# A hybrid decoder layer on one Trainium2 core: the last contraction block of the MLP's second matmul goes from plain products to seven products, and row ends move into the last product

## The chip, the cores and the metric

The kernel runs on one core of one Trainium2 chip. A core has TensorE (PE in the profile; its weight loads are PEld), VectorE (DVE), ScalarE (ACT), GpSimd (POOL) and SyncE (SP), which issues all DMAs here. PE writes its results to PSUM, of which the kernel uses eight banks of 128 partitions x 512 float32. The metric is device time in microseconds (us): the median of several executions. A profile is one more execution, taken by the hardware profiler; its span runs from the first to the last instruction.

## What is computed

One decoder layer for 1024 tokens of width 1024, all in float32. The first half (attention heads beside a gated recurrence, an output projection, a residual) is not touched by the change. The second half is the MLP:

```python
h = rmsnorm(x, mlp_pre_norm)
ff = square(relu(h @ w_ff1)) @ w_ff2        # (1024 x 1024) @ (1024 x 4096), then (1024 x 4096) @ (4096 x 1024)
x = x + rmsnorm(ff, mlp_post_norm)          # rmsnorm: y = v * rsqrt(mean(v*v) + 1e-6) * gain, row by row
```

## The kernel before

**Float32 by three passes.** Every float32 operand is split into two numbers that PE can multiply at full rate: `hi` is a copy by ACT (L83), `lo = src - hi` a subtraction by DVE (L84). A product is then three matmuls, hi x hi, hi x lo and lo x hi (`three_pass`, L86 to L89), each 128 x 128 weights against up to 512 columns.

**Seven products.** Both MLP matmuls use the Strassen-Winograd scheme: a 2 x 2 block product costs 7 block products and some block sums, not 8. The 4096 rows of `w_ff2` are eight "pairs" of 512 rows, numbered 0 to 7. For pairs 1 to 7 the first layer leaves seven left operands (blocks of the activation and their sums, made by POOL in `act_sums`) in DRAM, `act_dram[u]`, at the places `APLACE`. For pair 0 it leaves only the plain blocks (`act_plain` writes them to `act_raw`).

**Units.** A unit is one product `p` (1 to 7) of one pair: 4 row blocks x 2 contraction blocks x 3 passes = 24 matmuls (`mm2`). `GROUPS` lists the pairs that add up in the same PSUM banks: pair 1 alone, then 2, 3, 4, then 5, 6, 7. For each group the products run in the order `ORDER` (`LAST` for the last group), and for each product the pairs of the group one after the other. Four banks hold the four row blocks of a product; after its last unit `collect` takes them out: in group 0 ACT copies them to SBUF (`acc[p]`, L1640), in the others DVE adds them to `acc[p]` (L1644, L1642).

**What a unit needs.** `a_load` brings the left operand from DRAM (tile `ar`, 512 KB), `prep` splits it (`ah`, `al`) and the right one (`bh`, `bl`); `prep_sum` forms the right operand of products 5, 6, 4 and 7, one DVE operation each (L1582, L1588), from raw blocks of `w_ff2` (tile `br`, 1 MB each, two per pair; `b_load`, started by `b_pump` as buffers come free). In iteration `n` the code issues the load for unit n+3, the splits of n+2, the sum of n+4, then the matmuls of n, then a `collect` if the product ends. Each engine works strictly in this order. All second-layer tiles come from two arenas: `small` (30 slots of 128 x 1024 float32) and `large` (slots of 128 x 2048); a slot is handed out in the order in which slots were given back, and the user waits for the last reader of the old tile.

**Folding.** The seven collected sums must be combined into the four blocks of the result: C11 in `acc[2]`, C12 in `acc[3]`, C21 in `acc[4]`, C22 in `acc[7]`. These are the `fold_in` calls (L1649) in the table `at_last`, which hangs further work on the units of the last group.

**The end.** Pair 0 is multiplied plainly after the last unit: for each of the 8 row tiles and each half of the columns, 4 contraction blocks x 3 passes into a fresh bank (tile `fe`), 192 matmuls in all; its operands are loaded and split in `at_last` (`plain_load`, `plain_split`). Behind each row tile comes the row end: DVE adds the bank to `acc` (L1786), ACT squares and sums it (L1787), POOL makes the mean and the power -0.5 (L1791, L1799, L1800), DVE multiplies by the gain (L1761), and one tile later multiplies by the row's scale and adds the residual `x2r` (L1756); SP stores the row. The last tile does its second half in two quarters (L1777 to L1783).

**The first layer around it.** `ff1(q)` runs pair q = 0 to 15 of `w_ff1` by seven products; `act_store(q)` sends pair q's results to `act_dram`, two stores on SP that wait for POOL. `start2` prepares the first units during the last pair; `b_pump(-1)` and two `a_load` stand before it.

Of the kernel before, what the change touches and what calls it, by code (L numbers as in the profile page):

```python
# [35 lines left out]
def hymba_layer(ctx, tc, x, w_in, w_out, w_ff1, w_ff2, g_pre, lb_logits, g_mix, g_post,  # L36
# [1120 lines left out]
    act_raw = dp.tile([P, 2, 2, 2, 512], F32, name="actr")  # L1157
    act_dram = {u: dp.tile([P, 7, 2, 512], F32, name=f"actd{u}") for u in range(1, NPAIR // 2)}
# [145 lines left out]
    def act_plain(q):  # L1304

        l = lay.pop(q)
        nc.sync.dma_start(out=act_raw[:, q, 0, 0], in_=l["E1"][:, 0])
        nc.sync.dma_start(out=act_raw[:, q, 0, 1], in_=l["X"][:, 0])
        nc.sync.dma_start(out=act_raw[:, q, 1], in_=l["E1"][:, 1:3])
        drop(l["E1"], l["X"])  # L1310

# [180 lines left out]
    def ff1(q, between=None):  # L1492
# [9 lines left out]
        for p in EARLY if q in EARLY_PAIRS else STEADY if nq else FINAL:  # L1502
# [40 lines left out]
    GROUPS = ((1,), (2, 3, 4), (5, 6, 7))  # L1543
    NG = len(GROUPS)
    APLACE = {1: 0, 2: 1, 4: 2, 5: 3, 6: 4, 7: 5, 3: 6}
# [5 lines left out]
    acc = {}  # L1551

    def a_load(n):
        if n < n_units:
# [9 lines left out]

    b_queue = [(g, h, m) for g in range(NG) for m in range(2) for h in range(len(GROUPS[g]))]

    def b_pump(g):

        spare = sum((g, h) not in tt for h in range((len(GROUPS[g]) + 1) // 2)) if g >= 0 else 0
        while b_queue and b_queue[0][0] <= g + 1 and len(large.free) > spare:  # L1570
            b_load(*b_queue.pop(0))

# [3 lines left out]
    def b_source(g, p, h):  # L1576
# [7 lines left out]
        if p == 5 and h % 2 == 0:  # L1584
            tt[g, h // 2] = large.get(f"tt{g}{h}")
        t = tt[g, h // 2][:, 2 * (h % 2):2 * (h % 2) + 2]
        in0, in1 = {5: (b12, b11), 6: (b22, t), 4: (t, b21)}[p]
# [5 lines left out]
    def prep_sum(n):  # L1593
        if n < n_units:
            g, p, h = units[n]
            bsrc[n] = b_source(g, p, h)
            if g == NG - 1 and p == 4:
                drop(braw.pop((g, h, 1)))

    def prep(n):  # L1600
        if n >= n_units:
            return
# [20 lines left out]
    cur = []  # L1623

    def mm2(n, i, first, last):
        (ah, al), (bh, bl) = aop[n], bop[n]
        c = slice(i * P, (i + 1) * P)
        for j in range(2):
            three_pass(cur[i], (ah[:, j, c], al[:, j, c]), (bh[:, j], bl[:, j]), first and j == 0, last and j == 1)
# [4 lines left out]
    def collect(g, p, i):  # L1634

        pm = cur[i]
# [4 lines left out]
        elif g == NG - 1 and p == 4:  # L1641
            V.tensor_tensor(out=acc_at(p, i), in0=acc_at(p, i), in1=pm, op=ALU.subtract)  # L1642
# [4 lines left out]
    def fold_in(p, o, j, op=ALU.add):  # L1647

        V.tensor_tensor(out=acc[p][j], in0=acc[o][j], in1=acc[p][j], op=op)  # L1649
# [26 lines left out]
    b_pump(-1)  # L1676
# [7 lines left out]
    x2r, plain, praw = {}, {}, {}  # L1684

    def load_x2(t):
        if t < NT:
            x2r[t] = small.get(f"x2r{t}")
            nc.sync.dma_start(out=flat(x2r[t]), in_=x2_dram[t])

    def plain_load(kind, q):
        t = praw[kind, q] = large.get(f"{kind}p{q}")
        if kind == "w":
            src = w_ff2[2 * q * P:(2 * q + 2) * P].rearrange("(j p) c -> p j c", j=2)
        else:
            src = act_raw[:, q].rearrange("p j a c -> p j (a c)")
        nc.sync.dma_start(out=t.rearrange("p (j a) c -> p j (a c)", j=2), in_=src)

    def plain_split(kind, q, j):
        if j == 0:  # L1700
            plain[kind, q] = [large.get(f"{kind}p{x}{q}", F32R) for x in "hl"]
        hi, lo = (x[:, 2 * j:2 * j + 2] for x in plain[kind, q])
        split_into(hi, lo, praw[kind, q][:, 2 * j:2 * j + 2])
        if j == 1:
            drop(praw.pop((kind, q)))

    def plain_op(kind, q, j, c0, n):
        return tuple(x.rearrange("p (j a) c -> p j (a c)", j=2)[:, j, c0:c0 + n] for x in plain[kind, q])
# [3 lines left out]
        0: lambda: plain_load("w", 0),  # L1712
        1: lambda: plain_load("w", 1),
        3: lambda: fold_in(6, 1, 0),
        4: lambda: fold_in(6, 1, 1),
        5: lambda: plain_split("w", 0, 0),
        6: lambda: [fold_in(2, 1, 0), plain_split("w", 0, 1)],
        7: lambda: [fold_in(2, 1, 1), drop(*acc.pop(1))],
        8: lambda: plain_split("w", 1, 0),
        10: lambda: plain_split("w", 1, 1),  # L1720
        11: lambda: plain_load("a", 0),
        12: lambda: [fold_in(7, 6, 0), fold_in(6, 5, 0)],
        13: lambda: [fold_in(7, 6, 1), fold_in(6, 5, 1)],
        15: lambda: [fold_in(3, 6, 0), plain_split("a", 0, 0)],
        16: lambda: [fold_in(3, 6, 1), drop(*acc.pop(6)), plain_split("a", 0, 1), plain_load("a", 1)],
        18: lambda: [fold_in(4, 7, 0, ALU.subtract), plain_split("a", 1, 0), load_x2(0)],
        19: lambda: [fold_in(4, 7, 1, ALU.subtract), plain_split("a", 1, 1), load_x2(1)],
        20: lambda: [load_x2(2), load_x2(3)],
    }
    for n, (g, p, h) in enumerate(units):  # L1730
        final, nh = g == NG - 1, len(GROUPS[g])
        a_load(n + 3) if n else None
        prep(n + 2) if n else None
        prep_sum(n + 4)
        if h == 0:
            cur = [banks.get(f"f2{g}{p}{i}") for i in range(4)]
        b_pump(g)
        if final:
            at_last.get(n - n_last, lambda: None)()
        for i in range(4):  # L1740
            mm2(n, i, h == 0, h == nh - 1)
# [5 lines left out]
        if h == nh - 1:  # L1747
            for i in range(4):
                collect(g, p, i)


    def end_out(t, pieces, rf):

        xr = x2r.pop(t)
        for j, c in enumerate(pieces):
            V.scalar_tensor_tensor(c, c, rf, xr[:, j], op0=ALU.mult, op1=ALU.add)  # L1756
            nc.sync.dma_start(out=out[t * P:(t + 1) * P, j * 512:(j + 1) * 512], in_=c)
        drop(xr)

    def norm_gain(pieces, j):  # L1760
        V.tensor_tensor(out=pieces[j], in0=pieces[j], in1=gend[:, j], op=ALU.mult)  # L1761

    late = None
    for t in range(NT):
        pieces = [acc_at(p, t % 4) for p in ((2, 3) if t < 4 else (4, 7))]
        ss, rf = [col(f"fss{j}") for j in range(2)], col("frf")
        last = t == NT - 1
        for j, c in enumerate(pieces):
            pm = banks.get(f"fe{t}{j}")
            for i in range(4):  # L1770
                three_pass(pm, plain_op("a", i // 2, i % 2, t * P, P), plain_op("w", i // 2, i % 2, j * 512, 512),
                           i == 0, i == 3)
            fd = half(f"fd{t}{j}")
            if last and j:
                norm_gain(pieces, 0)
# [97 lines left out]
```

## Time and profile before

| | us |
|---|---|
| three runs | 1264.53, 1264.64, 1265.26 |
| median | 1264.64 |
| the profiled execution | 1262.62 |
| its span | 1260.6 |
| second layer, first to last matmul, of it | 943.8 to 1253.0 |

The profile groups instructions by line, engine and shape: `xN` is their number, then the busy time, the mean duration of one in ns, and the idle time of the engine before them with what ended it. The durations of matmuls overlap, so what one costs is the distance between starts. Rows of the timeline give start, duration, engine, line, operation, output and inputs. Rows of windows give for each stretch the busy time and number of instructions of PE, PEld, DVE, ACT and POOL, PE's granted clock, the mean busy share of the DMA engines and GB/s. "A <- B" among the waits is A waiting for B: us in total, times, longest.

### The profile page before, as it was taken

Reading aid. Unit: us, or ns where it says so; the run is one execution under the profiler, and the core shown is the slowest. Engines: PE = TensorE matmul, PEld = TensorE weight load, DVE = VectorE, ACT = ScalarE, POOL = GpSimd, SP = SyncE. Lnnn points to the kernel's source line nnn. Section 1 sums busy time; section 2 is a strip of 40 time slices with the busy share of each in tenths; the row PEclk is TensorE's granted clock in tenths of the full one; section 3 lists DMA queues with packets and bytes.
Section 4 is the critical chain, followed back from the end, with each engine's and each line's share of the span. In section 5 each row is a group of like instructions: output and inputs, shape, how many; then the busy total and the mean of one; then the engine's idle time right before and its main releaser. Section 6 shows DMA issues by size and latency. Waiting matters only on the chain. (4 is left out here: it accounts for less than half of the span.)

```text
span 1260.6 us, 17260 instructions
## 1 busy us (share of the span) xinstructions
PE 1235.9 (98%) x6512; PEld 1055.5 (84%) x6512; DVE 886.4 (70%) x1535; ACT 531.8 (42%) x970; POOL 300.9 (24%) x303
## 2 busy tenths in 40 slices
PE   9999999999999998999999999999999999999997
PEld 8898989888888887878878788888878888888886
DVE  5686868575666667668769756666675777698966
ACT  7623232222555556665565322222236444344412
POOL 0000000012222224046250487656621000000012
PEclk9999999999999999999999999999999999999999
DMA  5201111122322223235242545435368454424423
GB/s 210 68 18 51 34 51 34 35 84 64 88 70 82 69 83 109 103 134 183 96 155 77 207 167 184 148 133 180 142 253 324 164 201 134 160 92 133 163 88 117
DMA packets 58578, 153.98 MB, mean 122 GB/s; under 512 B 4992, under 2 KB 12928, under 8 KB 58240
## 3 DMA queue, kind: packets, MB, share of 16 engines
q1 hardware_dynamic: 58496, 152.89, 35.3%
q8 instruction: 51, 0.84, 0.3%
q14 instruction: 31, 0.25, 0.1%
HBM read 106.73 MB, written 39.85 MB: 116 GB/s over the span
## 5 line engine op out<-in xcount | busy, mean ns | idle before, releaser
L89 PE MATMUL f<-bh,al 128*128 128x512 f32 x392 | 152.6, 389 | 0.0
L88 PE MATMUL f<-bl,ah 128*128 128x512 f32 x392 | 152.6, 389 | 0.0
L87 PE MATMUL f<-bh,ah 128*128 128x512 f32 x392 | 152.6, 389 | 0.0
L84 DVE TENSOR_TENSOR al<-ar,ah 128x1024 fp32r<-128x1024 f32 x49 | 60.6, 1237 | 47.9 <-ACT ah L83 17.5
L89 PEld LDWEIGHTS f<-bh,al 128*128 128x128 f32 x392 | 73.6, 188 | 15.4
L88 PEld LDWEIGHTS f<-bl,ah 128*128 128x128 f32 x392 | 73.6, 188 | 15.3
L87 PEld LDWEIGHTS f<-bh,ah 128*128 128x128 f32 x392 | 73.6, 188 | 15.1
L83 ACT ACTIVATE ah<-ar 128x1024 fp32r<-128x1024 f32 x49 | 52.1, 1064 | 49.1 <-PE f L89 17.6
L1791 POOL TENSOR_SCALAR fp<-fss 128x1 f32<-128x1 f32 x8 | 3.7, 461 | 269.4 <-ACT fd L1787 269.4
L719 DVE TENSOR_TENSOR ptl<-pt,pth 128x512 fp32r<-128x512 f32 (+2 forms) x96 | 50.4, 552 | 23.0 <-ACT pth L718 22.7
L718 ACT ACTIVATE pth<-pt 128x512 fp32r<-128x512 f32 (+2 forms) x96 | 43.4, 486 | 41.2 <-PE pt L715 39.8
L691 DVE CUSTOM_DVE_ANT_0 p<-ps,bt 128x512 f32<-128x512 f32 (+2 forms) x84 | 44.4, 553 | 18.9 <-PE ps L689 18.7
L1290 POOL TENSOR_TENSOR e<-x,e 128x512 f32<-128x512 f32 x14 | 20.7, 1475 | 136.8 <-DVE x L1241 136.8
L79 POOL TENSOR_SCALAR ms<-hss 128x8 f32<-128x8 f32 x4 | 0.8, 198 | 209.1 <-DVE hss L552 209.1
L702 ACT ACTIVATE p<-p,nm 128x128 f32<-128x128 f32 (+3 forms) x64 | 49.4, 772 | 2.6 <-DVE nm L695 2.1
L83 ACT ACTIVATE bh<-br 128x1024 fp32r<-128x1024 f32 x28 | 29.8, 1063 | 43.5 <-PE f L89 38.2
L715 PE MATMUL pt<-ident,p 128*128 128x128 f32 x288 | 42.6, 275 | 4.5 <-DVE ptl L719 2.3
L748 POOL TENSOR_TENSOR anat<-anat,rd 128x128 f32<-128x128 f32 x32 | 14.5, 454 | 129.5 <-DVE anat L747 122.6
L715 PEld LDWEIGHTS pt<-ident,p 128*128 128x128 f32 x288 | 33.4, 140 | 9.0 <-DVE ptl L719 4.0
L732 PE MATMUL pov<-pth,v 128*128 128x256 f32 (+1 forms) x160 | 40.3, 287 | 0.0
L1644 DVE TENSOR_TENSOR acc<-f,acc 128x512 f32<-128x512 f32 x52 | 33.8, 684 | 8.3 <-PE f L89 8.3
L83 ACT ACTIVATE bh<-tt 128x1024 fp32r<-128x1024 f32 x21 | 22.3, 1060 | 38.5 <-PE f L89 23.1
(1622 smaller groups left out, 3904.4 us busy)
## 6 DMA issues: line engine op xcount, KB each, us to landing
ar<-actd SPq DMA_DIRECT2D x49, 512.0 KB, 3.5
raw<-in_w_in_dram SPq DMA_DIRECT2D x28, 512.0 KB, 3.6
w1r<-in_w_ff_dram SPq DMA_DIRECT2D x14, 1024.0 KB, 6.3
br<-in_w_ff_dram SPq DMA_DIRECT2D x14, 1024.0 KB, 7.8
actd<-e SPq DMA_DIRECT2D x17, 768.0 KB, 4.0
actd<-e SPq DMA_DIRECT2D x11, 1024.0 KB, 4.0
xr<-in_x_dram SPq DMA_DIRECT2D x8, 512.0 KB, 8.7
raw<-in_w_out_dram SPq DMA_DIRECT2D x8, 512.0 KB, 3.4
```

The costliest lines, as they stand in the source:

```text
L83: S.activation(hi, src, AF.Copy)
L84: eng.tensor_tensor(out=lo, in0=src, in1=f32(hi), op=ALU.subtract)
L87: TE.matmul(dst, lhs[0], rhs[0], start=start, stop=False)
L88: TE.matmul(dst, lhs[0], rhs[1], start=False, stop=False)
L89: TE.matmul(dst, lhs[1], rhs[0], start=False, stop=stop)
L691: V.tensor_tensor_reduce(out=pe[:, k0:k0 + n], in0=pS[:, :n], in1=bts[hd][:, o:o + n], scale=1.0, scalar=-3.0e38, op0=ALU.add, op1=ALU.max ...
L702: S.activation(pe[:, :nk], pe[:, :nk], AF.Exp, bias=nm[:, b:b + 1], accum_out=dn[:, b:b + 1])
L715: TE.transpose(pt[:, j * P:(j + 1) * P], pe[:, jj * P:(jj + 1) * P], ident)
L718: S.activation(hi, src, AF.Copy)
L719: V.tensor_tensor(out=lo, in0=src, in1=f32(hi), op=ALU.subtract)
L732: TE.matmul(po[:, c0:256], vst, pt[j // 4][q][:, j % 4, c0:], start=j == 0 and q == 0, stop=j == nj - 1 and q == 1)
L1644: V.tensor_tensor(out=acc_at(p, i), in0=pm, in1=acc_at(p, i), op=ALU.add)
```

## The change

Pair 0 joins the seven-product scheme, and the groups become two of four pairs.

- `act_plain` writes pair 0's plain blocks into `act_dram[0]`. The four operand sums of pair 0 are made later, during first-layer pairs 6 to 10, by `late_sums`: four loads, four DVE operations, four stores. `act_dram[0]` has an eighth place for the block from which they start.
- `GROUPS` becomes (1, 2, 3, 0) and (4, 5, 6, 7): 56 units and no plain block. Group 0 is collected by ACT, so products run over four pairs with no DVE addition there.
- In the last group, products 6, 2, 3 and 4 do not start in fresh banks: `seed` lets ACT copy an already folded sum into the four banks, and the matmuls add to it. The folding order in `at_last` changes to match.
- Products 2 and 3 of the last group are finished from the banks: `row_half` squares and sums on ACT and multiplies by the gain on DVE.
- The last product runs by row block, not by pair: all four pairs for row block 0, then 1, 2, 3 (24 matmuls each), so that the operands of its four units must all be ready at its start; `DEEP` moves loads and splits of the last ten units further ahead. Row ends (`row_out`, `row_half`, `row_scale2`) stand between the blocks. The last block is done in two column halves, 48 matmuls of 256 columns, the second half in a bank of its own (`tail_bank`).
- `b_pump` gets limits (`most`, `hold`) that keep slots free; the next unit's A load moves behind the split of the unit before it; product 4's sum changes sign, so that DVE always adds.

```diff
-    act_raw = dp.tile([P, 2, 2, 2, 512], F32, name="actr")
-    act_dram = {u: dp.tile([P, 7, 2, 512], F32, name=f"actd{u}") for u in range(1, NPAIR // 2)}
+    act_dram = {u: dp.tile([P, 7 if u else 8, 2, 512], F32, name=f"actd{u}") for u in range(NPAIR // 2)}
...
+    def late_sums(q):
+
+        def bring(dst, place_):
+            nc.sync.dma_start(out=dst, in_=act_dram[0][:, place_])
+
+        def make(dst, in0, in1, op, place_):
+            V.tensor_tensor(out=dst, in0=in0, in1=in1, op=op)
+            nc.sync.dma_start(out=act_dram[0][:, place_], in_=dst)
...
             if nq and p == 4:
                 w1_split(nq, 1)
+                late_sums(q)
...
-    GROUPS = ((1,), (2, 3, 4), (5, 6, 7))
+    GROUPS = ((1, 2, 3, 0), (4, 5, 6, 7))
...
+    def b_pump(g, most=99, hold=0):
+
+        while b_queue and b_queue[0][0] <= g + 1 and most > 0:
+            k, _, m = b_queue[0]
+            spare = hold + sum((q, h) not in tt_open for q in range(max(g, 0), k + m) for h in range(2))
+            if len(large.free) <= spare:
+                break
             b_load(*b_queue.pop(0))
+            most -= 1
...
+    def seed(p, src):
+
+        seeded[p] = [banks.get(f"f2s{p}{i}") for i in range(4)]
+        for i in range(4):
+            S.activation(seeded[p][i], acc_at(src, i), AF.Copy)
...
         if p == 2:
             for b in ("B11", "B21"):
                 large.add("A", 2)
+            b_pump(-1, hold=3)
             prep_sum(0)
             prep_sum(1)
...
-    b_pump(-1)
+    b_pump(-1, most=2)
...
+    def row_half(t, j, src, dst):
+
+        S.activation(half(f"fd{t}{j}"), src, AF.Square, accum_out=sums[j][:, t:t + 1])
+        V.tensor_tensor(out=dst, in0=src, in1=gend[:, j], op=ALU.mult)
...
+    def row_out(t, order=(0, 1)):
+        xr = x2r.pop(t)
+        for j in order:
+            c = acc_at(((2, 3), (4, 7))[t // 4][j], t % 4)
+            V.scalar_tensor_tensor(c, c, scale[:, t:t + 1], xr[:, j], op0=ALU.mult, op1=ALU.add)
+            nc.sync.dma_start(out=out[t * P:(t + 1) * P, j * 512:(j + 1) * 512], in_=c)
+        drop(xr)
...
+        4: lambda: fold_in(2, 1, 0),
+        5: lambda: fold_in(2, 1, 1),
+        8: lambda: fold_in(3, 5, 0),
+        9: lambda: fold_in(3, 5, 1),
+        10: lambda: [seed(6, 1), drop(*acc.pop(1))],
+        12: lambda: fold_in(4, 7, 0),
+        13: lambda: [fold_in(4, 7, 1), seed(2, 2)],
+        14: lambda: fold_in(7, 5, 0),
+        15: lambda: [fold_in(7, 5, 1), drop(*acc.pop(5))],
+        16: lambda: fold_in(3, 6, 0),
+        17: lambda: [fold_in(3, 6, 1), seed(3, 3)],
+        18: lambda: [fold_in(4, 6, 0), fold_in(7, 6, 0)],
+        19: lambda: [fold_in(4, 6, 1), fold_in(7, 6, 1), drop(*acc.pop(6))],
+        21: lambda: [seed(4, 4), second_blocks(4, 5)],
+        22: lambda: second_blocks(6, 7),
     }
+    DEEP = n_units - 10
...
-        a_load(n + 3) if n else None
-        prep(n + 2) if n else None
+        if n:
+            for k in range(n + 2, n + (5 if n == n_units - 5 else 4 if n >= DEEP else 3)):
+                a_load(k)
+                prep_sum(k)
+                prep(k)
+            a_load(n + 3)
+            if n + 1 >= DEEP:
+                a_load(n + 4)
...
+                if final and p in (2, 3):
+                    row_half(i, p - 2, cur[i], acc_at(p, i))
+                    (row_base if p == 2 else row_scale2)(i, p - 2)
+                    drop(cur[i])
...
+    for i in range(4):
+        t = 4 + i
+        if i < 3:
+            for h in range(4):
+                mm2(n0 + h, i, cur[i], False, h == 3)
+            if i < 2:
+                row_out(2 * i)
+                row_out(2 * i + 1)
+                load_x2(4 + 2 * i)
+                load_x2(5 + 2 * i)
             else:
+                row_out(5)
+            row_half(t, 0, cur[i], acc_at(4, i))
+            row_scale2(t, 0)
+            if i == 1:
+                row_out(4)
+            continue
...
+        for h in range(4):
+            mm2(n0 + h, i, tail_bank[:, lo], False, h == 3, 256, 256)
+        more, ms = col("fmore"), col("fms")
+        S.activation(half("fdhi")[:, lo], tail_bank[:, lo], AF.Square, accum_out=more)
+        V.tensor_tensor(out=dst[:, hi], in0=tail_bank[:, lo], in1=gend[:, 0, hi], op=ALU.mult)
+        V.tensor_scalar(ms, more, 1.0 / D, more0, op0=ALU.mult, op1=ALU.add)
+        G.tensor_tensor(out=scale[:, t:t + 1], in0=ms, in1=nhalf[:, :1], op=ALU.pow)
+        row_out(t, (1, 0))
```

More of the change, by code (lines that the diff above doesn't have):

```diff
@@ L1565, in hymba_layer @@
     b_queue = [(g, h, m) for g in range(NG) for m in range(2) for h in range(len(GROUPS[g]))]
-    def b_pump(g):
-        spare = sum((g, h) not in tt for h in range((len(GROUPS[g]) + 1) // 2)) if g >= 0 else 0
-        while b_queue and b_queue[0][0] <= g + 1 and len(large.free) > spare:
+    tt_open = set()
+    def b_pump(g, most=99, hold=0):
[4 more added lines that the diff above has]
+                break
             b_load(*b_queue.pop(0))
+            most -= 1
     def block(g, h, m, a):
@@ L1683, in hymba_layer @@
     nc.sync.dma_start(out=flat(gend), in_=g_mlp_post.partition_broadcast(P))
-    x2r, plain, praw = {}, {}, {}
+    x2r = {}
+    sums = (ssq0, rstd0)
+    scale, base = gpre, lbl.rearrange("p h l -> p (h l)")
     def load_x2(t):
[L1687 to L1708, printed above, removed]
+        x2r[t] = small.get(f"x2r{t}")
@@ L1711, in hymba_layer @@
     at_last = {
[L1712 to L1722, printed above, removed]
@@ L1734, in hymba_layer @@
         prep_sum(n + 4)
         if h == 0:
-            cur = [banks.get(f"f2{g}{p}{i}") for i in range(4)]
-        b_pump(g)
+            cur = seeded.pop(p) if p in seeded else [banks.get(f"f2{g}{p}{i}") for i in range(4)]
+            fresh_banks = not (final and p in (6, 2, 3))
+        b_pump(g, hold=int(n == 0))
         if final:
```

143 lines of the change are left out of this document (68 added, 75 removed).

## The prediction

> **What bounds the kernel now.** I read the page's first lines, then the waits of the matmul engine in the half that the change touches, then windows by stage.
>
> ```profile
> span 1260.6 us, 17260 instructions
> PE 1235.9 (98%) x6512; PEld 1055.5 (84%) x6512; DVE 886.4 (70%) x1535; ACT 531.8 (42%) x970; POOL 300.9 (24%) x303
> ```
>
> ```profile
> PE f115a L1222 <- ACT x L1244: 0.7, 1, 0.7
> ```
>
> ```profile
> 744.00:934.00 190.00, 189.31 (x835) 156.45 (x834) 124.53 (x132) 47.88 (x63) 120.65 (x82) 1.00 0.46 168
> 944.00:960.00 16.00, 16.00 (x72) 13.23 (x72) 8.72 (x7) 6.46 (x10) 6.08 (x4) 1.00 1.03 415
> 960.00:1160.00 200.00, 200.00 (x884) 165.66 (x883) 149.92 (x148) 94.80 (x102) 0.00 (x0) 1.00 0.46 157
> 1160.00:1200.00 40.00, 40.00 (x178) 33.11 (x178) 37.83 (x38) 16.44 (x16) 0.00 (x0) 1.00 0.45 157
> ```
>
> The second fence is the only wait of PE from 700 us to the end: 0.7 us, in the first layer. In the windows (length, then busy time of PE, PEld, DVE, ACT, POOL, then clock, DMA share, GB/s) PE is busy all the time and at full clock, even in 1160 to 1200 us, where DVE is busy 37.83 of 40 us. So the second layer lasts as long as its matmuls, and then there is a tail. DVE at 95% has not cost PE anything, but it is the next bound, and the 944 to 960 us window shows the DMA engines full.
>
> The profiled execution took 1262.62 us, 2.0 more than its span; the three runs have a median of 1264.64. I work on the span and move the difference onto the median, taking a change of over 0.2% (2.5 us) as what a measurement can tell from none.
>
> **The matmuls.** The spacing, not the 389 ns of a row, is what one costs:
>
> ```profile
> L87 PE MATMUL fe<-wph,aph x64: 388/389/390, 1209.7 to 1252.5; 128*128 128x512 f32 x64
> L87 PE MATMUL f<-bh,ah x391: 388/389/390, 943.8 to 1209.0; 128*128 128x512 f32 x196
> ```
>
> The plain block (tile fe) has 64 triples, 192 matmuls; from its first to its last L87 lie 63 triples in 42.8 us: 42.8 / 189 = 0.2265 us each. The change drops these 192 and adds pair 0 as a seven-product pair: 7 units of 4 row blocks x 2 x 3 = 24, so 168. Net 24 fewer: **-5.44 us**. A unit is 24 x 0.2265 = 5.44 us. The first unit starts at 943.8 in both kernels.
>
> The last row block of the last product is computed in two column halves: 24 matmuls of 512 columns become 48 of 256. The first layer has that shape:
>
> ```profile
> 126.01 0.28 PE L87 MATMUL pig<-wig2h,hTh 128*128 128x256 f32 x1
> ...
> 127.09 0.28 PE L87 MATMUL pig<-wig2h,hTh 128*128 128x256 f32 x1
> ```
>
> ```profile
> 126.13 0.19 PEld L89 LDWEIGHTS pig<-wig2h,hTl 128*128 128x128 f32 x1
> ```
>
> Nine steps lie between the two matmuls: 1.08 / 9 = 0.120 us. So the halves cost 48 x 0.120 - 5.44 = **+0.32 us**. The weight load of 0.19 us starts at 126.13, while the matmul of 126.01 still runs.
>
> The Trainium skill (TensorE: Matmul & The Clock Gate, Part 3, The mechanism) says that a weight load overlaps running matmuls only when its row group differs; all of these use the whole array. By that rule the halves pay load plus stream, and I price it as a rival; the row above contradicts it.
>
> **The tail.** Before and after, the kernel ends with a chain from the last matmul to the last two output rows:
>
> ```profile
> 1252.99 0.39 PE L89 MATMUL fe<-wph,apl 128*128 128x512 f32 x1
> ```
>
> ```profile
> 1253.42 0.42 DVE L1777 TENSOR_TENSOR acc<-fe,acc 128x256 f32<-128x256 f32 x1
> ...
> 1255.11 0.21 DVE L1799 TENSOR_SCALAR fms<-fss,fmore 128x1 f32<-128x1 f32 x1
> 1255.24 0.68 DVE L1761 TENSOR_TENSOR acc<-acc,gend 128x512 f32<-128x512 f32 x1
> 1256.36 1.42 DVE L1756 SCALAR_TENSOR_TENSOR acc<-acc,frf,x2r 128x512 f32<-128x512 f32 x2 [0.44 <-POOL frf L1800]
> ```
>
> ```profile
> 1253.96 0.42 ACT L1778 ACTIVATE fd<-acc 128x256 f32<-128x256 f32 x1 [1.75 <-DVE acc L1777]
> 1254.28 0.19 ACT L1778 ACTIVATION_READ_ACCUMULATOR fd<-acc 128x1 f32 x1
> ```
>
> ```profile
> 1249.68 0.68 POOL L1799 TENSOR_SCALAR fms<-fss,fp 128x1 f32<-128x1 f32 x1 [2.36 <-ACT fd L1787]
> 1250.45 0.55 POOL L1800 TENSOR_TENSOR frf<-fms,nhalf 128x1 f32<-128x1 f32 x1
> ...
> 1255.47 0.86 POOL L1800 TENSOR_TENSOR frf<-fms,nhalf 128x1 f32<-128x1 f32 x1 [2.71 <-DVE fms L1799]
> ```
>
> From the start of the last matmul (1252.99) to the two output rows (1256.36) are 3.37 us. After the change the bank already holds the earlier sums, so nothing is added on DVE: the last half matmul takes 0.28; 0.04 to hand over (1252.99 + 0.39 to 1253.42); ACT squares the half straight from the bank, 0.51 (1253.96 to 1254.28 + 0.19); about 0.10 to hand over (my estimate from the gaps in these rows); one small DVE operation until POOL starts, 0.36 (1255.11 to 1255.47); the power on POOL; 0.03. With 0.55 for the power that is 1.87 us, a gain of 1.50. The last matmul now starts only 0.120 before its stream ends and not 0.2265, which gives back 0.11. So **-1.39 us** with the power at 0.55 and -1.08 at 0.86. The 0.86 stood beside the multiplication of 1255.24; afterwards DVE waits idle there. I take -1.2. If the shorter chain brings nothing, the term is 0.
>
> The Trainium skill (SBUF — State Buffer, Who interferes with whom) says that a DVE instruction with two SBUF inputs contends with a GpSimd instruction that reads SBUF. The two durations agree with it, and by it the power takes 0.55 and the term is -1.39.
>
> Sum: -5.44 + 0.32 - 1.2 = **-6.3 us**, if PE nowhere waits. The rest of this part is whether it does.
>
> **DVE in the second layer.** The groups and the spacing on DVE:
>
> ```profile
> L84 DVE TENSOR_TENSOR al<-ar,ah 128x1024 fp32r<-128x1024 f32 x49 | 60.6, 1237 | 47.9 <-ACT ah L83 17.5
> L83 ACT ACTIVATE ah<-ar 128x1024 fp32r<-128x1024 f32 x49 | 52.1, 1064 | 49.1 <-PE f L89 17.6
> L1644 DVE TENSOR_TENSOR acc<-f,acc 128x512 f32<-128x512 f32 x52 | 33.8, 684 | 8.3 <-PE f L89 8.3
> L1649 DVE TENSOR_TENSOR acc<-acc,acc 128x1024 f32<-128x1024 f32 x14 | 17.0, 1217 | 0.1
> ```
>
> ```profile
> 1179.00 1.22 DVE L84 TENSOR_TENSOR bl<-br,bh 128x1024 fp32r<-128x1024 f32 x1
> 1180.14 1.22 DVE L1588 TENSOR_TENSOR tt<-tt,br 128x1024 f32<-128x1024 f32 x1
> 1181.27 1.22 DVE L1649 TENSOR_TENSOR acc<-acc,acc 128x1024 f32<-128x1024 f32 x1
> ```
>
> Operations of 1024 columns follow each other every 1.135 us. A unit needs two (2.27), a product in four of seven one more for its sum. Group 0 now has no collection on DVE (ACT does it): under 3.5 of 5.44 us. Against before, the change takes eight plain splits and 36 of the 52 bank additions of the L1644 group off DVE, and adds 14 splits, 4 sums and 4 late sums.
>
> The dense place is products 2 and 3 of the last group, 8 units or 43.5 us. DVE's order there holds 10 unit splits (the last product is wanted whole at its start, so its splits are pulled forward), 22.7; 4 sums, 4.5; 6 folds, 6.8; 12 multiplications by the gain, 0.62 each, 7.4. Together 41.4 us, 95%, as much as 1160 to 1200 us carried without a wait of PE. It enters with two units ready. The tightest operand is that of the last unit, 55, wanted three quarters into the first row block of the tail: 8 x 5.44 + 18 x 0.2265 = 47.6 us after the start of unit 44. Its A load takes a slot that unit 50 frees, at 38.1; with
>
> ```profile
> ar<-actd SPq DMA_DIRECT2D x49, 512.0 KB, 3.5
> br<-in_w_ff_dram SPq DMA_DIRECT2D x14, 1024.0 KB, 7.8
> actd<-e SPq DMA_DIRECT2D x17, 768.0 KB, 4.0
> x2r<-x2d SPq DMA_DIRECT2D x8, 512.0 KB, 4.6
> ```
>
> it lands at 41.6, two copies on ACT and the last subtraction on DVE bring 45. DVE's own queue: 0.7 for the last collection of product 6, 38.9 of work ahead of that point, about 3 lost where the seeds of product 3 stand on ACT ahead of a split and wait for a fold, and some 2.5 of waits for banks and squares (both my estimates, of three copies of an ACT row each): 45. Margin 2.6 us; I cost it at nothing, between 0 and +4.
>
> **Row ends.** In the tail DVE has 7 rows x 1.42 and four multiplications, about 13 us, in 4 x 5.44 us of matmuls; each x2 load (4.6) is issued a row block ahead. Rows 0 to 3 hide behind blocks 4 and 5, rows 4 to 6 behind 6 and 7: nothing. Without cover, rows 5 and 6 at the end cost 2.8.
>
> **First layer.** The late sums are four DVE operations of 1.22 us in four different pairs, and eight DMAs on SP behind the weight load of each pair; DVE has 65 us free in 744 to 934. Uncovered they would cost 4.9, and twice that beside POOL's work; no matmul waits for what stands behind them in the next few us, so nothing. The stores of pairs 0 and 1 only change their target.
>
> **The start of the second layer.** Now four pairs' first blocks, not one pair's two, must be there for units 0 to 3 (units 2 and 3 start at 943.8 + 10.9 = 954.7 and at 960.1). Two are loaded early as before; the other two stand on SP behind the store of pair 14:
>
> ```profile
> 930.73 0.37 SPq L1301 DMA_DIRECT2D actd<-e  x1
> ...
> 939.05 5.00 SPq L1563 DMA_DIRECT2D br<-in_w_ff_dram  x6
> ...
> 953.55 0.37 SPq L1301 DMA_DIRECT2D actd<-e  x1
> ```
>
> By the order of the slots they take pair 14's buffers, free 4.0 after that store, at 934.7: landed at 942.5, split by 945, ten us early. The six loads of 939.05 that filled the DMA engines now become two. Nothing.
>
> **Rivals.**
>
> *DVE falls behind in products 2 and 3.* The 1.135 becomes 1.22 (+2.9 on 41.4), or the last A load is late by as much: the margin of 2.6 is used up, and PE waits 2 to 6 us in the last product. For it: 95% load and ACT's seeds in the same queue as its splits. Against: 1160 to 1200 us. Time at 4 us: 1264.64 - 2.3 = 1262.3.
>
> *Row ends pile up at the end*, because x2 loads or outputs hold SP: the uncovered 2.8 us, 1261.1. Against it: each load stands a row block ahead, and 4.6 is less than 5.44.
>
> *The start of the second layer stalls* (slower). If the two block loads get slots that pair 15 frees, they wait on SP for its store: 953.55 + 4.0 + 7.8 = 965.3, split at 967.6, and unit 3 waits 7.5 us, about 9 if the two loads share the engines. It decides from a slot later than 950 (960.1 - 7.8 - 2.3). -6.3 + 9 = +2.7: 1267.3. For it: SP goes strictly in order, and the 944 to 960 window was full. Against: pair 14's slots come first in the list.
>
> *Weights loaded between the streams.* The halves then take 48 x (0.19 + 0.120) = 14.9 instead of 5.8 us: +9.1, 1267.4. Against it stands the row at 126.13. It is what the rule of the Trainium skill (TensorE: Matmul & The Clock Gate) named above would do here.
>
> **How the numbers follow.** Forecast 0.71, with its own range 1257.5 to 1260.5; DVE behind 0.10; row ends 0.06; start stalls 0.11; weights 0.02. Predicted 1264.64 - 6.3 = **1258.3 us** (a span of 1254.3). Faster by over 0.2% (under 1262.1) is the forecast, the row ends and a third of the DVE case: 0.80; within 0.2% the rest of that case: 0.07; slower 0.13. Range 1257.0 (the whole tail gain and a little spread) to 1263.5 (into the DVE case).
>
> **What would show it.** Right: no wait of PE on an operand after 944 us; first unit near 943.8; 1320 matmuls of 512 and 48 of 256 columns at 0.2265 and 0.120; under 2 us from the start of the last matmul to the last row's output; power near 0.55. Wrong: PE waiting on bl or al in the last product, on br at units 2 and 3, or rows 5 and 6 after the last matmul.

## The result and the profile after

| | kernel before, us | changed kernel, us |
|---|---|---|
| first timing, median | 1264.70 (4 runs) | 1257.51 (4 runs, 1256.67 to 1258.58) |
| ratio, 95% interval | | 0.9947, 0.9934 to 0.9960 |
| second timing, median | 1263.30 (9 runs) | 1256.75 (5 runs) |
| ratio, 95% interval | | 0.9951, 0.9939 to 0.9963 |
| span of the profiled execution | 1260.6 | 1256.0 |

The change made the kernel 7.2 us faster, 6.55 us in a second timing on another occasion. The forecast was 6.3, or 1258.3 us; the measured 1257.51 lies inside its own range of 1257.5 to 1260.5, at the very edge.

The page's first lines of the changed kernel, then its only wait of PE from 700 us on:

```profile
span 1256.0 us, 17242 instructions
PE 1230.4 (98%) x6512; PEld 1053.0 (84%) x6512; DVE 863.8 (69%) x1490; ACT 544.9 (43%) x995; POOL 308.8 (25%) x304
```

```profile
PE f115a L1222 <- ACT x L1244: 0.7, 1, 0.7
```

It is the same wait as before, of the same length. So the new second layer has PE busy without a gap, and what is to be explained is the length of its stream and its tail. The two spans cannot be compared whole: the code up to the last first-layer product (tile f115c) is reached by the same instructions on PE in both kernels, and its first matmul starts at

```profile
L1222 PE MATMUL f115c<-B220h,wf x2: 389/389/389, 940.4 to 941.1; 128*128 128x512 f32 x2
```

in the kernel before and at

```profile
L1222 PE MATMUL f115c<-B220h,wf x2: 389/389/389, 941.8 to 942.5; 128*128 128x512 f32 x2
```

in the changed one. Over all profiles of kernels that are the same up to there it lies between 940.0 and 942.1. Most of this spread goes with a fall of the clock in the first half, which some executions have and others not: the granted clock from 486 to 502 us was 0.89 in the profiles with a start of 940.6 to 942.1, and 1.00 in those with 940.0 to 940.8. Kernels that are the same up to there fall on both sides, so the spread has nothing to do with the change, and I read every run from that start to the end of its span: **320.2 us before, 314.2 after, 6.0 less**. What the medians show beyond that lies within their intervals.

The end of the matmul stream and of the tail, on PE and then on DVE, ACT and POOL:

```profile
1243.73 0.28 PE L1663 MATMUL f2s<-bh,ah 128*128 128x256 f32 x1
...
1249.36 0.28 PE L1663 MATMUL f2tail<-bh,al 128*128 128x256 f32 x1
```

```profile
1246.40 1.42 DVE L1748 SCALAR_TENSOR_TENSOR acc<-acc,gpre,x2r 128x512 f32<-128x512 f32 x2 [0.99 <-DMA x2r<-x2d]
...
1250.27 0.42 DVE L1851 TENSOR_TENSOR acc<-f2tail,gend 128x256 f32<-128x256 f32 x1 [2.12 <-ACT fdhi L1850]
1250.61 0.20 DVE L1852 TENSOR_SCALAR fms<-fmore,fmore 128x1 f32<-128x1 f32 x1
1251.48 1.41 DVE L1748 SCALAR_TENSOR_TENSOR acc<-acc,gpre,x2r 128x512 f32<-128x512 f32 x2 [0.67 <-POOL gpre L1853]
```

```profile
1249.76 0.39 ACT L1850 ACTIVATE fdhi<-f2tail 128x256 f32<-128x256 f32 x1 [2.42 <-PE f2tail L1663]
1250.04 0.19 ACT L1850 ACTIVATION_READ_ACCUMULATOR fdhi<-f2tail 128x1 f32 x1
```

```profile
1250.90 0.55 POOL L1853 TENSOR_TENSOR gpre<-fms,nhalf 128x1 f32<-128x1 f32 x1 [2.95 <-DVE fms L1852]
```

The 48 half matmuls take 47 steps from 1243.73 to 1249.36, 0.120 us each, as the 256-column matmuls of the first layer did. From tile f115c to the last matmul are 307.6 us, against 312.6 before: 5.0 less. From the last matmul's start to the last row's output are 2.12 us, against 3.37: 1.25 less. From there to the end of the span are 4.5 us, 0.3 more than before.

The tightest operand, that of unit 55, and the A load it waits for, on DVE and ACT:

```profile
1223.39 1.22 DVE L1622 TENSOR_TENSOR tt<-br,tt 128x1024 f32<-128x1024 f32 x1
1226.79 1.23 DVE L84 TENSOR_TENSOR al<-ar,ah 128x1024 fp32r<-128x1024 f32 x1 [2.17 <-ACT ah L83]
1227.93 1.22 DVE L84 TENSOR_TENSOR bl<-tt,bh 128x1024 fp32r<-128x1024 f32 x1
```

```profile
1225.69 1.06 ACT L83 ACTIVATE ah<-ar 128x1024 fp32r<-128x1024 f32 x1 [3.66 <-DMA ar<-actd]
```

The last product starts 72 matmuls before 1243.73, at 1227.41, and wants this operand 18 matmuls later, at 1231.49. The split ends at 1229.15: 2.3 us to spare. DVE itself had been idle for 2.17 us before it, waiting for the load; unit 44 started 192 matmuls before the last product, at 1183.9, so ACT's copy of the load began 41.8 us after it.

The start of the second layer, on SP (SPq: its DMA issues):

```profile
932.37 0.37 SPq L1301 DMA_DIRECT2D actd<-e  x1
932.83 4.08 SPq L1591 DMA_DIRECT2D br<-in_w_ff_dram  x2
937.00 0.89 SPq L1585 DMA_DIRECT2D ar<-actd  x2
```

The two further block loads follow pair 14's store at once and do not wait for pair 15's; unit 2's split ends on DVE at 947.9, and the unit starts at 944.5 + 10.9 = 955.4.

### The profile page after: what moved, and what is told of

It reads as the page before. It is cut to its first block, busy times and chain, and to the rows that moved or that the text cites. A ratio compares the mean times of both kernels' runs of the same rounds, so it can differ in the third digit from the quotient of the medians.

```text
span 1256.0 us, 17242 instructions
## 1 busy us (share of the span) xinstructions
PE 1230.4 (98%) x6512; PEld 1053.0 (84%) x6512; DVE 863.8 (69%) x1490; ACT 544.9 (43%) x995; POOL 308.8 (25%) x304
## 5 line engine op out<-in xcount | busy, mean ns | idle before, releaser
L84 DVE TENSOR_TENSOR al<-ar,ah 128x1024 fp32r<-128x1024 f32 x56 | 70.6, 1261 | 80.5 <-ACT ah L83 78.2
L1663 PE MATMUL f<-bh,ah 128*128 128x512 f32 x320 | 124.5, 389 | 0.0
L1663 PE MATMUL f<-bl,ah 128*128 128x512 f32 x320 | 124.5, 389 | 0.0
L1663 PE MATMUL f<-bh,al 128*128 128x512 f32 x320 | 124.5, 389 | 0.0
L1663 PEld LDWEIGHTS f<-bl,ah 128*128 128x128 f32 x320 | 60.1, 188 | 12.6
L1663 PEld LDWEIGHTS f<-bh,al 128*128 128x128 f32 x320 | 60.1, 188 | 12.4
L1663 PEld LDWEIGHTS f<-bh,ah 128*128 128x128 f32 x320 | 60.1, 188 | 12.4
L718 ACT ACTIVATE pth<-pt 128x512 fp32r<-128x512 f32 (+2 forms) x96 | 43.4, 486 | 41.8 <-PE pt L715 40.4
L1663 PE MATMUL f2s<-bh,al 128*128 128x512 f32 (+1 forms) x128 | 48.9, 382 | 0.0
L1663 PE MATMUL f2s<-bl,ah 128*128 128x512 f32 (+1 forms) x128 | 48.9, 382 | 0.0
L1663 PE MATMUL f2s<-bh,ah 128*128 128x512 f32 (+1 forms) x128 | 48.9, 382 | 0.0
```

Source lines behind the costliest of these rows:

```text
L84: eng.tensor_tensor(out=lo, in0=src, in1=f32(hi), op=ALU.subtract)
L718: S.activation(hi, src, AF.Copy)
L1663: TE.matmul(pm, a[:, j, c], b[:, j, d], start=start and j == 0 and q == 0, stop=stop and j == 1 and q == 2, skip_group_check=True)
```

## The experiments

The stretch is the time from the first matmul of tile f115c to the end of the span, the chain that from the last matmul's start to the last row's output. e1 to e10 are one execution each; where one kernel was profiled twice (changed and e11, e4 and e12), the two stretches agree to 0.1 us.

| run | f115c starts at | span ends at | stretch | PE waits in it | chain |
|---|---|---|---|---|---|
| before | 940.4 | 1260.6 | 320.2 | 0 | 3.37 |
| changed | 941.8 | 1256.0 | 314.2 | 0 | 2.12 |
| e1, 24 matmuls left out | 941.8 | 1250.5 | 308.7 | 0 | 2.12 |
| e2, no seeds | 940.6 | 1264.1 | 323.5 | 0.2 | 10.95 |
| e10, no seeds, other order | 941.5 | 1258.5 | 317.0 | 0 | 4.87 |
| e3, last block whole | 941.1 | 1255.4 | 314.3 | 0 | 2.68 |
| e4, scale first | 940.0 | 1253.9 | 313.9 | 0 | 1.86 |
| e5, 4.5 us more on DVE | 941.7 | 1256.2 | 314.5 | 0 | 2.12 |
| e6, 9.1 us more on DVE | 940.8 | 1262.5 | 321.7 | 4.2 | 2.11 |
| e7, normal lead | 941.8 | 1255.9 | 314.1 | 0 | 2.12 |
| e8, 18 us more on SP | 940.0 | 1264.7 | 324.7 | 7.3 | 2.12 |
| e9, late sums four times | 948.6 | 1262.7 | 314.1 | 0 (4.8 before it) | 2.11 |
| e11, changed again | 942.1 | 1256.3 | 314.2 | 0 | 2.12 |
| e12, scale first again | 940.3 | 1254.2 | 313.9 | 0 | 1.86 |

### Is the second layer as long as its matmuls? (e1)

```diff
-        for i in range(4):
+        for i in range(0 if n == 13 else 4):
             mm2(n, i, cur[i], fresh_banks and h == 0, h == nh - 1)
```

> The changed kernel without the 24 matmuls of one unit (the second unit of product 6 in the first group, pair 2): its splits, sums, loads and copies stay, so this part of the result is missing from the output. I read times from the first matmul of the last first-layer product (tile f115c) to the end of the span: 320.2 us in the kernel before, 314.2 in the changed kernel. Theory (the second layer lasts as long as its matmuls, 0.2265 us each): 314.2 - 5.4 = 308.8. Rival (loads, splits or DVE set the pace as much as PE does): less than 3 us gained, because the operands of the later units are not ready any sooner.

308.7: 5.5 us less for 24 matmuls less. Loads and splits did not hold the later units back. This is the term of -5.44 measured by itself, on 24 other matmuls.

### What do the seeds do? (e2, e10)

```diff
-        10: lambda: [seed(6, 1), drop(*acc.pop(1))],
+        10: lambda: fold_in(6, 1, 0),
+        11: lambda: [fold_in(6, 1, 1), drop(*acc.pop(1))],
...
-                    row_half(i, p - 2, cur[i], acc_at(p, i))
+                    collect(g, p, cur[i], i)
+                    row_half(i, p - 2, acc_at(p, i), acc_at(p, i))
...
-            row_half(t, 0, cur[i], acc_at(4, i))
+            V.tensor_tensor(out=acc_at(4, i), in0=cur[i], in1=acc_at(4, i), op=ALU.add)
+            row_half(t, 0, acc_at(4, i), acc_at(4, i))
```

> The changed kernel without seeds: products 6, 2, 3 and 4 of the last group start in fresh banks, the folded sums are added by DVE afterwards (two folds and four plus four plus five bank additions more on DVE, 16 copies fewer on ACT), and the squares are taken from SBUF. Theory: DVE has about 4.5 us to spare before the last product (2.2 idle before the last split, 2.3 from that split to its first use), product 2's four additions are 2.5 of it, so PE still does not wait; the chain behind the last matmul gets an addition of 0.4 and a handover, so 314.2 + 0.5 to 1.5 = 314.7 to 315.7. Rival (the seeds are what keeps DVE in time): PE waits on bl or al in the last product and the stretch is 318 or more.

323.5 us, 3.3 more than the kernel before. The theory's number missed. The rival's (318 or more) came, but not in its way: PE waited only 0.2 us for bl, and from tile f115c to the last matmul are 308.1 us, against 307.6, so the matmuls were not what got longer. DVE, last product of the last group, in the run without seeds:

```profile
1230.75 0.69 DVE L1682 TENSOR_TENSOR acc<-f,acc 128x512 f32<-128x512 f32 x1
1232.29 0.69 DVE L1734 TENSOR_TENSOR acc<-acc,gend 128x512 f32<-128x512 f32 x1 [0.85 <-ACT fd L1733]
...
1239.33 2.74 DVE L1748 SCALAR_TENSOR_TENSOR acc<-acc,gpre,x2r 128x512 f32<-128x512 f32 x4
...
1259.64 1.41 DVE L1748 SCALAR_TENSOR_TENSOR acc<-acc,gpre,x2r 128x512 f32<-128x512 f32 x2 [0.67 <-POOL gpre L1856]
```

The last matmul started at 1248.69, and the last row went out 10.95 us later. The first rows started at 1239.33, in the changed kernel at 1231.46. Each row half went addition on DVE, square on ACT, multiplication in place on DVE, and DVE stood 0.85 us in each. My estimate had counted the additions and not these round trips. The next run kept the additions and took most round trips away (the diff is against the run without seeds):

```diff
-                    row_half(i, p - 2, acc_at(p, i), acc_at(p, i))
+                    row_square(i, p - 2, acc_at(p, i))
...
+            for i in range(4 if final and p in (2, 3) else 0):
+                row_gain(p - 2, acc_at(p, i))
...
+            if i:
+                row_gain(0, acc_at(4, i - 1))
```

> The kernel without seeds again, with another order on DVE: all four additions of a product first, then its multiplications by the gain, and in the last product the multiplication of a row block behind the next block's matmuls. The run without seeds took 323.5 us from tile f115c to the end, not the 314.7 to 315.7 I expected: PE waited 0.2 us, as expected, but the row ends came 9 us late, because each went addition, square on ACT, multiplication, with DVE idle 0.85 us in each of the eight. Theory (that round trip, not the additions, was the price): with it gone the last row ends 2.5 to 5 us after the last matmul in place of 11, 315 to 317 in all. Rival (the additions themselves fill DVE): still over 320.

317.0, with no wait of PE: 6.5 us came from the order alone. DVE in the tail of this run still shows round trips in the last product, two whole ones of 0.85 us of which this is the first, and two of half the width (0.63 and 0.66):

```profile
1236.39 0.68 DVE L1843 TENSOR_TENSOR acc<-f,acc 128x512 f32<-128x512 f32 x1
1237.92 0.69 DVE L1740 TENSOR_TENSOR acc<-acc,gend 128x512 f32<-128x512 f32 x1 [0.85 <-ACT fd L1737]
```

So the seeds are worth 2.8 us against the better of the two orders without them (317.0 - 314.2), and up to 9.3 against the plain one. Half of what the change gains hangs on them, and none of it through the matmuls: they keep the row ends from piling up behind the last one.

### The halves and the last chain (e3, e4)

```diff
-        lo, hi = slice(0, 256), slice(256, 512)
...
+        for h in range(4):
+            mm2(n0 + h, i, cur[i], False, h == 3)
+        row_out(6)
+        row_half(t, 0, cur[i], acc_at(4, i))
```

> The changed kernel with its last row block in one piece: 24 matmuls of 512 columns, one square, one multiplication, one scale. Theory: the matmuls get 0.32 us shorter, the last one ends 0.11 later, and the chain to the last row's output goes from 2.12 us to about 2.8 (a whole square 0.8 in place of 0.59, a whole multiplication 0.69 in place of 0.42, before the scale): 314.2 + 0.2 to 0.6. Rival (the weight loads of the halves do not overlap, so that the halves cost far more than 0.32): the stretch gets shorter by over 1 us.

314.3, 0.1 more, where 0.2 to 0.6 were expected. The chain grew from 2.12 to 2.68, of which the shorter stream gives back 0.32 and 0.11: 0.13 is left. The halves gain hardly anything, and the rival with separate weight loads, which would have shown over 1 us the other way, falls.

```diff
+        V.tensor_scalar(ms, more, 1.0 / D, more0, op0=ALU.mult, op1=ALU.add)
         V.tensor_tensor(out=dst[:, hi], in0=tail_bank[:, lo], in1=gend[:, 0, hi], op=ALU.mult)
-        V.tensor_scalar(ms, more, 1.0 / D, more0, op0=ALU.mult, op1=ALU.add)
```

> The changed kernel with two DVE instructions of the tail exchanged: the small one that makes the row's mean stands ahead of the last multiplication by the gain. In the changed kernel that multiplication started 0.51 us after the square, behind it, and the mean behind that. Theory: the mean does not wait for the multiplication any more, the power on POOL starts 0.3 us earlier and the multiplication runs beside it: from the last matmul's start to the last row's output 2.12 becomes 1.75 to 1.85. Rival (the multiplication beside POOL's power makes the power longer, as in the kernel before, 0.86 in place of 0.55): nothing is gained, 2.05 to 2.15.

The chain went to 1.86, the length that the prediction had worked out (1.87). DVE and POOL of this run:

```profile
1248.51 0.21 DVE L1851 TENSOR_SCALAR fms<-fmore,fmore 128x1 f32<-128x1 f32 x1 [1.91 <-ACT fdhi L1850]
1248.64 0.41 DVE L1852 TENSOR_TENSOR acc<-f2tail,gend 128x256 f32<-128x256 f32 x1
1249.40 1.42 DVE L1748 SCALAR_TENSOR_TENSOR acc<-acc,gpre,x2r 128x512 f32<-128x512 f32 x2 [0.34 <-POOL gpre L1853]
```

```profile
1248.81 0.55 POOL L1853 TENSOR_TENSOR gpre<-fms,nhalf 128x1 f32<-128x1 f32 x1 [2.41 <-DVE fms L1851]
```

The multiplication (one input from SBUF, the other from PSUM) ran beside the power, and the power stayed at 0.55. The 0.86 of the kernel before stood beside a multiplication with two SBUF inputs. Both agree with the rule of the Trainium skill that the prediction cites (SBUF — State Buffer, Who interferes with whom). One more POOL operation of the tail shows the same: the mean of the last row's first half (tile fmore) took 0.27 us in e1, e5 and e12, where DVE had no row output (L1748, two SBUF inputs) beside it, and 0.51 to 0.79 in the changed kernel, e4, e7, e9 and e11, where it had one. Timed beside the changed kernel:

> The changed kernel itself, timed in five rounds. Theory (a gain of 6.0 us in the second layer and its tail; what the profiles show beyond it is spread of the untouched first 940 us, 1.8 us over the runs so far): 6.0 us, a ratio of 0.9953, within 0.9945 to 0.9961. Rival (the whole 7.2 us of the medians belongs to the change): 0.9943 or less.

> The changed kernel with the last scale ahead of the last multiplication (it took 0.26 us from the last chain in its first look), timed beside the changed kernel. Theory: 0.3 us faster than the changed kernel, less than the two can be told apart by; ratio to the kernel before 0.9950, within 0.9942 to 0.9959. Rival (the single time of 1255.68 was the kernel's own, not the spread's): 1.5 us or more below the changed kernel.

The changed kernel took 1256.75 us (ratio 0.9951, 0.9939 to 0.9963), the one with the scale first 1256.66 (0.9949, 0.9935 to 0.9963). The 0.3 us can be seen in the profile and not in the times; it is the only edit that was better than the change, by an amount that no timing here shows.

### How much slack does DVE have at the end? (e5, e6, e7)

```diff
-        22: lambda: second_blocks(6, 7),
+        22: lambda: [second_blocks(6, 7), burn(8)],
...
+    def burn(k):
+        for _ in range(k):
+            V.tensor_tensor(out=acc[3][0], in0=acc[3][0], in1=acc[3][0], op=ALU.max)
```

The diff is that of e6; in e5 it is burn(4).

> The changed kernel with four more DVE operations of 1024 columns (4.5 us; they take the maximum of a tile with itself, so no value changes) just ahead of the splits of units 54 and 55. Theory: DVE waits 2.2 us for the last A load there and the last split ends 2.3 us before its first use, together 4.5, so PE waits 0 to 0.5 us and the stretch from tile f115c to the end stays at 314.2 to 314.7. Rival 1 (DVE is at its limit, every us on it is one on PE): 318.7. Rival 2 (far more slack than that): no wait, like the theory; the run with eight tells them apart.

> As the run before with eight such operations, 9.1 us. Theory (4.5 us of slack): PE waits about 4.5 us in the first row block of the last product, 314.2 + 4.5 = 318.7. Rival 1 (no slack): 323.3. Rival 2 (slack of 9 us or more, because the row block order of the last product wants its operands late): 314.2 to 314.7.

With four the list of waits shows none, and the stretch is 314.5 us. The 0.3 lies where unit 55's operand is first used: at 1231.40 two steps of PE take 0.41 and 0.33 us in place of 0.227. So these 4.5 us used the slack up. With eight PE waits:

```profile
PE f2s L1663 <- DVE bl L84: 3.4, 2, 2.9
PE f2s L1663 <- ACT bh L83: 0.8, 1, 0.8
```

4.2 us, where 4.5 were expected. From the first run the slack is 4.5 - 0.3 = 4.2, from the second 9.1 - 4.2 = 4.9: the 4.5 us are confirmed from both sides. But the stretch grew by 7.5 and not by 4.2. The rest is PE's speed after the gap:

```profile
1236.55 0.63 PE L1663 MATMUL f2s<-bh,al 128*128 128x512 f32 x1
1236.97 0.63 PE L1663 MATMUL f2s<-bh,ah 128*128 128x512 f32 x1
```

0.42 between starts in place of 0.2265, from 1236 to 1240.4.

```diff
-    DEEP = n_units - 10
+    DEEP = n_units
```

> The changed kernel without the earlier loads and splits of the last ten units: the normal lead of two units, and the last unit of product 3 brings the splits of three units. Theory: DVE does the same work before the last product, in another order, and more slots of the small arena are free for the A loads; PE waits 0 to 1.5 us, the stretch from tile f115c to the end is 314.2 to 315.7. Rival (the last product by row blocks needs the deeper lead): PE waits for the last units' operands by at least the two splits that are moved, 4.5 us, 318.7 or more.

314.1, no wait: the deeper lead is worth nothing here. The rival falls.

### How much slack does the start have? (e8)

```diff
             b_pump(-1, hold=3)
+            for _ in range(3):
+                for h in (2, 3):
+                    rows = w_ff2[GROUPS[0][h] * 4 * P:(GROUPS[0][h] + 1) * 4 * P].rearrange("(j m p) c -> m p j c", j=2, m=2)
+                    nc.sync.dma_start(out=braw[0, h, 0].rearrange("p (j a) c -> p j (a c)", j=2), in_=rows[0])
```

> The changed kernel with the two raw block loads that stand on SP behind the store of pair 14 done three more times each into the same buffers, every one waiting for the one before: some 18 us of delay on SP at the start of the second layer, ahead of the A loads of units 2 and 3. In the changed kernel unit 2's split ended 7.5 us before its unit began and unit 3's about as early. Theory (7 to 10 us of slack there, then every us of delay is one on PE): PE waits 6 to 11 us for units 2 and 3, and the stretch from tile f115c to the end is 320 to 325. Rival (the start is covered by the last first-layer pair, or the delay is taken up by later units): under 317.

324.7, with these waits of PE at unit 2:

```profile
PE f L1663 <- ACT bh L83: 6.6, 1, 6.6
PE f L1663 <- DVE bl L84: 0.7, 1, 0.7
```

Unit 2's split ends 21.7 us after the start of tile f115c, 15.6 later than in the changed kernel (6.1). 7.3 us of this come through as waits, inside the expected 6 to 11, and again 3.2 us more as slow matmuls behind the gap. So loads that come late there do make PE wait, as the slower rival of the prediction says, and each such wait costs more than its length; the rival's condition, a slot that comes late, did not hold.

### Are the late sums hidden? (e9)

```diff
             V.tensor_tensor(out=dst, in0=in0, in1=in1, op=op)
+            for _ in range(3):
+                V.tensor_tensor(out=dst, in0=dst, in1=dst, op=ALU.max)
```

> The changed kernel with each of the four late sums of pair 0 followed by three more DVE operations of the same size (the maximum of the tile with itself, no value changes): 12 more in first-layer pairs 7 to 10, each 1.1 to 2.3 us. Theory (the late sums are hidden under the matmuls, DVE has 65 us free in that layer): no new wait of PE there; from the first matmul of tile f17a to the first of tile f115c, and from there to the end (314.2), nothing changes. Rival (what they delay is on the path): the stretch of pairs 7 to 10 grows by up to 14 us.

The theory failed here. Tile f115c starts at 948.6, some 7 us late, and PE waits in the first layer:

```profile
PE f110d L1222 <- DVE x L1257: 3.2, 1, 3.2
PE f111d L1222 <- DVE x L1257: 1.6, 1, 1.6
```

Only the last two of the four places cost anything. POOL, DVE and ACT between two rounds of pairs 9 and 10:

```profile
819.13 2.14 POOL L1290 TENSOR_TENSOR e<-x,e 128x512 f32<-128x512 f32 x1 [8.98 <-DVE x L1241]
...
827.79 1.29 POOL L1178 TENSOR_TENSOR ss<-ss,w1r 128x512 f32<-128x512 f32 x1
...
841.66 2.12 POOL L1290 TENSOR_TENSOR e<-x,e 128x512 f32<-128x512 f32 x1 [8.98 <-DVE x L1241]
```

```profile
829.11 1.06 ACT L83 ACTIVATE ws10h<-ss 128x1024 fp32r<-128x1024 f32 x1 [5.64 <-POOL ss L1178]
```

```profile
831.45 2.31 DVE L1320 TENSOR_TENSOR lsa<-lsd,lsa 128x1024 f32<-128x1024 f32 x1
833.79 3.75 DVE L1322 TENSOR_TENSOR lsa<-lsa 128x1024 f32<-128x1024 f32 x3
837.46 0.68 DVE L1264 TENSOR_TENSOR e<-f19b,x 128x512 f32<-128x512 f32 x1
```

This is a loop: DVE finishes a pair's results (x, L1241), POOL makes that pair's sums and then the next pair's weight sums (ss), ACT and DVE split those, then comes the late sum, and behind it on DVE the results of the next pair, from which POOL starts again. One round took 841.66 - 819.13 = 22.5 us, while PE needs 84 x 0.2267 = 19.0 for a pair. The first two rounds (773.61 to 796.71 and to 819.13) lost 7.4 us against PE without a wait, so the loop had at least that much lead; the third made PE wait. Without the three additional operations (833.79 to 837.46, 3.7 us) a round would be 18.9. That would leave one late sum per pair 0.2 us, but the late sum itself took 2.31 here. In the changed kernel it takes 1.21:

```profile
820.48 1.29 POOL L1178 TENSOR_TENSOR ss<-ss,w1r 128x512 f32<-128x512 f32 x1
```

```profile
822.79 1.05 ACT L83 ACTIVATE ws10h<-ss 128x1024 fp32r<-128x1024 f32 x1
```

```profile
826.39 1.21 DVE L1320 TENSOR_TENSOR lsa<-lsd,lsa 128x1024 f32<-128x1024 f32 x1
```

There POOL has finished ss at 821.77, 1.0 us before ACT takes it. So the loop has about 1.0 us left in a round, and a second late sum per pair (some 1.1 us) would by this estimate have used it up.

## Why the prediction was right

**The matmuls.** -5.44 for 24 of them, +0.32 for the halves and +0.11 for the later last start make -5.01. The profile has 5.0, and e1 takes the first term apart. No step of it failed. The start at 943.8 was 0.7 too late for the kernel before: its first matmul starts at 943.14, 1367 steps of 0.2266 before the last at 1252.99; the changed kernel's starts at 944.53. No term of the sum rests on it.

**The tail.** Forecast: a chain 1.50 shorter with the power at 0.55. Measured: the power at 0.55, the chain 1.25 shorter. So the sign "under 2 us" was missed, with 2.12. The cause is the last multiplication by the gain, which my chain left out, as if it ran beside the square: it started at 1250.27, when ACT had left the same bank at 1250.23, and put 0.34 us ahead of the mean; shorter hand-overs gave some of it back. e4 moves it behind the mean, and the chain is 1.86, against the 1.87 worked out. The taken -1.2 has the 0.11 in it, so it compares with 1.25 - 0.11 = 1.14. Another 0.3 is lost behind the last row's output. The last two stores took 2.0 us from issue to landing in both kernels, and the DMA engines moved nothing for over 1 us before them, so a fuller DMA queue is not the cause; what it is stays open.

**No wait of PE in the second layer.** Right, and with the right margins: 2.3 us where 2.6 were worked out for unit 55, DVE's slack confirmed by e5 and e6. The path was the A load (ACT's copy at 41.8 us, landing at 41.6 worked out); DVE's own queue, put at the same 45 us, was in fact 2.17 us ahead of it. The rival with DVE behind names the right place, and what it would take is some 4.5 us more on DVE.

**Row ends hidden.** Right, but for a reason that I did not give. I counted DVE's operations against the matmuls' time, and by that count the kernel without seeds would have been nearly as good. It was the seeds that took the round trip over ACT out of the row ends. The rival's mechanism was there too: in the last product DVE waited four times, 2.6 us in all, for an x2 load (0.99 us before the rows at 1246.40), and the stores took 5.5 us in the median to land, against 2.0 before. It cost nothing, because DVE still stood idle for 2.12 us before the last multiplication.

**Late sums at nothing.** The price was right: from tile f17a to tile f115c are 169.8 us before and 169.6 after. The reason was wrong: "DVE has 65 us free" says nothing about a loop over three engines, which had about one operation of room.

**The start.** Right: the two loads took pair 14's slots, and 7.5 us were left at unit 2 of the ten I had counted.

**The size.** 6.0 us in the profiles and 7.2 and 6.55 in the medians, against 6.3. That 1257.51 lies inside the range of 1257.5 to 1260.5 by 0.01 us is luck: the interval of the ratio reaches from 1256.4 to 1259.6. Of the difference in the profiles 0.06 us lie in the chain and 0.3 behind it.

## What to carry to other kernels

Where one engine is busy without a gap, the price of a change on it is the count of its instructions times their spacing, and the work lies in finding out whether the others keep up. For that, free time of an engine is the wrong measure: follow the loop or the round trip in which its instruction stands, and take the slack there. A value that another engine can put where the accumulation will find it saves not only the addition but the order that the addition forces.

## What the runs showed of the hardware that was not expected

A gap on PE costs more than its length. After gaps, from one matmul's start to the next, of 3.3 and 1.2 us (e6), 7.0 us (e8) and 3.6 us (e9) matmuls of 512 columns ran at 0.42 to 0.43 us for 3 to 4.5 us; after e9's second gap, of 2.0 us, they did not. The window of e9 in the slow stretch shows the granted clock (third value from the end):

```profile
844.00:847.00 3.00, 3.00 (x8) 2.32 (x8) 2.62 (x4) 1.55 (x2) 3.00 (x3) 0.50 0.79 308
```

Half clock, and it was 0.50 in the slow stretches of e6 and e8 too, so waits of 4.2 to 7.3 us cost 2.3 to 3.3 us more than their length. The Trainium skill (TensorE: Matmul & The Clock Gate, Part 1: The HAM clock gate) states a fall to half rate after an idle window of about 3.4 us, until another window is busy. The half clock agrees. The length does not quite: in e6 the profile shows PE idle for 2.92 us in the first gap, less than that window, and the granted clock was down to 0.89 in the microsecond from 1233 and to 0.50 in the next, when the second gap had hardly begun. Stalls should be priced with this, which my rivals were not.

ACT and DVE did not read one PSUM bank at the same time: in the changed kernel's tail the multiplication on DVE is released by ACT's square of the same bank (the bracket of its row above), 1250.27 against 1249.76, which is 0.51 us; in e3 the whole multiplication starts at 1249.48, released by the square that ran from 1248.76 to 1249.44. The rows show a wait that the program keeps. What the chip would do without it was not tried.
